# Dense attention: the value product in three float32r products with 512 moving columns

## The chip, the cores and the metric

The kernel runs on one core of a Trainium2 chip. A core has engines that run side by side, each with its own queue of instructions: TensorE (PE: matrix products and transposes; its weight loads are shown apart as PEld), VectorE (DVE), ScalarE (ACT), GpSimd (POOL), and SyncE (SP), which starts most transfers. They share the on-chip memory SBUF; PE writes into PSUM, eight banks of 512 fp32 columns by 128 partitions. The metric is the device time of one execution in microseconds (us), as the median of several runs.

## The reference

One encoder layer on 1,024 tokens with 1,024 features, all in float32: a normalisation, one projection, two attention mixers, an output projection, and a gated MLP with a convolution. The change lies in mixer A, dense attention with 8 query heads over 2 key/value heads of 64 features:

```
sc = jnp.einsum('bqkgd,bskd->bkgqs', qb, k, preferred_element_type=jnp.float32) * scale
p = jax.nn.softmax(sc, axis=-1)
return jnp.einsum('bkgqs,bskd->bqkgd', p.astype(v.dtype), v)
```

## The kernel before

All of SBUF is held in two arenas, `bigf` (float32) and `bigr` (float32r, a float32 that PE multiplies in a faster way with fewer bits), PSUM in one tile `ps`. A product that must keep float32's precision is made of float32r products: each operand is split into a high part (a copy that rounds to float32r) and a low part (the operand minus its high part), and high x high, high x low and low x high are added in PSUM.

The body is emitted twice, by `emit(True)` and, behind a condition, by `emit(False)`. The first is the bounded case: a bound on the scores, from the gains, lets the exponentials be taken without subtracting a row's maximum. With the given inputs the first alone runs to the end; the second is skipped.

Mixer A (`a_main`, from 210 to 391 us) is a loop over 16 groups `g`. A group is one block of 128 tokens by one key/value head with its 4 query heads, so 512 query columns. For each of 8 blocks `kt` of 128 keys, a step,

- two float32r products make the scores of 128 keys by 512 queries in a PSUM bank (L701, L702), four banks in turn;
- ACT takes their exponential into one of three slots of `bigf` (L704);
- two steps later, the value product (`pv`, L696): four float32 products, in each of which 128 query columns of the exponentials are the weights and 65 columns move, the 64 features of the value and a column of ones that yields the softmax's denominator. A float32 product is two instructions. The result lies with queries on partitions.

The last two value products of a group and its normalisation (`o_norm`, L721 and L722: DVE's reciprocal of the denominators and the product with them) are handed as `tail` to the next group and done in its first steps. `prep` brings the next group's queries: a split (L650 on ACT, L651 on DVE), then four transposes on PE (L182) and a copy out of PSUM on ACT (L667). `late` and `spread` put other work into the loop: in groups 0 and 1 what is left of the projection's rotary sums (DVE L433, L524, L527; POOL L294 and L517), in groups 5 to 9 mean squares for mixer B's queries (ACT L547, DVE L499, a root on ACT at L505 with a change of its function table), the preparation of output weights (ACT L955, DVE L960), fills (L1069); in groups 10 to 13 four normalisations (DVE L563, L564, then POOL's gain L530). Groups 14 and 15 also prepare mixer B (from L762 on).

Each instruction stands in the program in the order in which the functions are called; a scheduler then sets the order on every engine's queue, taking an instruction earlier or later by its own estimates of when the operands are ready. An engine works its queue in order. So the order around the change is found in the built program, not in the text of the kernel alone.

Of the kernel before, what the change touches and what calls it, by code (L numbers as in the profile page):

```python
# [14 lines left out]
AF = mybir.ActivationFunctionType  # L15
# [17 lines left out]
O_IDF = 0  # L33
# [93 lines left out]
def tile_encoder_layer(ctx, tc, x, w_in, gains, outg, norm1_g, norm2_g, w_out, w_up, conv_w, conv_b,  # L127
# [14 lines left out]
    def emit(bounded):  # L142
# [7 lines left out]
        def f(off, n):  # L150
            return bigf[:, off:off + n]
# [11 lines left out]
        def fp(off, *dims):  # L163
            return raw_ap(bigf[:, off:off + 1], dims)
# [49 lines left out]
        def qab(tt):  # L214
            return O_QAB + 1024 * tt
# [130 lines left out]
            act(rp(R_KHA + 256 * u, [128, 2], [1024, 2], [1, 128])[0:64], pb[0:64], AF.Copy)  # L346

        def v_fetch():
            gp.memset(fp(F_VA + 64, [66, 16]), 1.0)
            for kv in range(2):  # L350
                dma(fp(F_VA + 66 * kv, [132, 8], [1, 64]),
                    kvscr[:, :, 128 + 64 * kv:192 + 64 * kv].rearrange("t p c -> p t c"))

        def v_scale():

            vec.tensor_copy(f(SM_SS1, 1), f(SM_MC, 1))
            vec.tensor_copy(f(SM_SS1, 8), f(SM_R1, 8))
            for t in range(8):
                v = fp(F_VA + 132 * t, [66, 2], [1, 64])
                act(v, v, AF.Copy, scale=f(SM_SS1 + t, 1))  # L360

        def fill_k():
            for i in range(4):
# [320 lines left out]
            return [nat, first] + [lambda i=i: mx(i) for i in range(4)] + [last]  # L684

        def a_main(g, prep, tail, late, plan, late_plan):

            b, kv = divmod(g, 2)
            q2 = R_Q2A + 512 * (g % 2)
            ql = R_QLA + 512 * (g % 2)  # L690
            ob = 6 + g % 2
            slots = {}

            def pv(kt):
                for i in range(4):
                    mm(bank(ob, 65, 66 * i), f(slots[kt] + 128 * i, 128), f(F_VA + 132 * kt + 66 * kv, 65),  # L696
                       start=(kt == 0 and i == 0), stop=(kt == 7), skip_group_check=True)

            for kt in range(8):
                st = (2, 3, 0, 1)[kt % 4] if bounded else 2 + kt % 2  # L700
                mm(bank(st), r(R_K2A + 1024 * kv + 128 * kt, 128), r(q2, 512), start=True, stop=False)  # L701
                mm(bank(st), r(R_KHA + 1024 * kv + 128 * kt, 128), r(q2 if bounded else ql, 512), start=False, stop=True)  # L702
                slots[kt] = p_slots()[0]
                act(f(slots[kt], 512), bank(st), AF.Exp)  # L704
# [12 lines left out]
            return [lambda: pv(6), lambda: pv(7), lambda: o_norm(ob, 66, qab(b) + 256 * kv, ([64, 4], [1, 64]))]  # L717

        def o_norm(t, step, dst, dims):
# [507 lines left out]
            if g > 3 and fills:  # L1227
                fills.pop(0)(qab((g - 1) // 2) + 256 * ((g - 1) % 2))
        for t in tail:
            t()  # L1230
        take(prep, 99)

        first, steps_of = b_prep(1)
# [442 lines left out]
```

## Time and profile before

| | us |
|---|---|
| median of three runs | 1301.46 (1300.12 to 1302.01) |
| the profiled execution | 1300.51 |
| its span | 1298.7 |
| dense attention within it | 210 to 391 |

| engine | busy in the whole span | busy from 210 to 391 us |
|---|---|---|
| PE | 1236.4 | 181.00 |
| DVE | 908.5 | 41.16 |
| ACT | 637.4 | 101.81 |
| POOL | 391.8 | 23.22 |

The span is that of the engines' work; the execution's time has 1.8 us more around it. A row of a timeline gives start, duration, engine, line, what is written and read, and in brackets how long the engine had been idle and what ended that. Rows of one engine overlap: a matrix product is shown with its latency, so the distance from start to start is what one costs, and ACT and DVE begin an instruction before the last has ended where the two don't depend on each other. A row of groups gives count, busy time, mean ns of one and the idle time before it. A row of stretches gives the length, busy time and number of instructions of PE, PEld, DVE, ACT and POOL in that order, then the granted TensorE clock, the share of the DMA engines and GB/s.

### The profile page before, as it was taken

What the parts mean: (1) busy time and instruction counts of PE and PEld (TensorE: products, weight loads), DVE (VectorE), ACT (ScalarE), POOL (GpSimd) and SP (SyncE); (2) the same over time, 40 slices, a digit from 0 to 9 for tenths busy, and PEclk for the clock granted to TensorE, in tenths of its full rate; (3) what the DMA queues carried; (4) which work ended last, traced back from release to release, by engine and by line L of the source; (5) the groups of instructions that cost most, each with busy time, mean ns of one, the idle gap of its engine ahead of it and who ended that gap; (6) DMA issues with size and microseconds to landing.
All of it is one profiled execution on the core that took longest, in us unless ns stands there. A gap on an engine that the chain in (4) does not pass through costs nothing.

```text
span 1298.7 us, 18774 instructions
## 1 busy us (share of the span) xinstructions
PE 1236.4 (95%) x7063; PEld 1061.5 (82%) x7063; DVE 908.5 (70%) x1270; ACT 637.4 (49%) x1001; POOL 391.8 (30%) x300
## 2 busy tenths in 40 slices
PE   7999999999998889999999999999999998889996
PEld 7999998999997777888788888888888886657885
DVE  5988685124107779656999999999999964657672
ACT  7856554566556566535544453444443442234430
POOL 1610143000212230011465675665675530000000
PEclk9999999999999899999999999999999998999998
DMA  7126303000014444413222223232223357448970
GB/s 264 54 84 156 88 5 75 24 17 17 9 25 100 106 107 115 156 65 106 74 105 91 92 93 122 94 117 90 91 96 122 122 183 282 166 148 277 315 242 36
DMA packets 120935, 147.12 MB, mean 113 GB/s; under 512 B 51009, under 2 KB 79489, under 8 KB 120321
## 3 DMA queue, kind: packets, MB, share of 16 engines
q1 hardware_dynamic: 119617, 141.10, 33.6%
q0 software_dynamic: 1216, 4.72, 1.7%
q8 instruction: 57, 0.93, 0.3%
q14 instruction: 45, 0.37, 0.1%
HBM read 107.25 MB, written 33.82 MB: 109 GB/s over the span
## 4 chain that ended last, share of the span: by engine, by line
PE 55%; DVE 18%; issue 4%; DMA 4%; ACT 3%; POOL 1%; SPq 0%; ACTq 0%; DVEq 0%; POOLq 0%
PE ps L696 8%; PE ps L1349 6%; PE ps L1351 6%; PE ps L1350 6%; DVE bigf L1382 6%; PE ps L1481 4%; PE ps L1482 4%; PE ps L1480 4%; PE ps L701 3%; PE ps L702 2%; DVE bigf L1353 2%; PE ps L1004 2%; PE ps L1006 2%; PE ps L1005 2%; DVE bigr L1333 2%
## 5 line engine op out<-in xcount | busy, mean ns | idle before, releaser
L1349 PE MATMUL ps<-bigr 128*128 128x512 f32 x616 | 241.0, 391 | 6.5 <-DVE bigf L1353 5.9
L1350 PE MATMUL ps<-bigr 128*128 128x512 f32 x616 | 239.7, 389 | 0.0
L1351 PE MATMUL ps<-bigr 128*128 128x512 f32 x616 | 239.7, 389 | 0.0
L1382 DVE SCALAR_TENSOR_TENSOR bigf<-bigf 128x768 f32<-128x768 f32 (+1 forms) x176 | 178.8, 1074 | 26.5 <-ACT bigf L1380 26.4
L1332 ACT ACTIVATE bigr<-bigf 128x512 fp32r<-128x512 f32 x154 | 93.2, 625 | 139.3 <-POOL bigf L1324 70.4
L1460 ACT ACTIVATE bigr<-bigf 128x1024 fp32r<-128x1024 f32 x77 | 80.5, 1058 | 148.9 <-DMA bigf<-gscr 57.1
L1349 PEld LDWEIGHTS ps<-bigr 128*128 128x128 f32 x616 | 115.6, 188 | 35.1 <-DVE bigf L1353 9.3
L696 PEld LDWEIGHTS ps<-bigf 128*128 128x128 f32 x1024 | 131.9, 191 | 9.3 <-issue 0.3
L1351 PEld LDWEIGHTS ps<-bigr 128*128 128x128 f32 x616 | 115.6, 188 | 24.2
L1350 PEld LDWEIGHTS ps<-bigr 128*128 128x128 f32 x616 | 115.7, 188 | 23.5
L1461 DVE TENSOR_TENSOR bigr<-bigf,bigr 128x1024 fp32r<-128x1024 f32 x77 | 93.2, 1222 | 57.0 <-ACT bigr L1460 46.8
L1480 PE MATMUL ps<-bigr 128*128 128x512 f32 x308 | 114.1, 401 | 16.6 <-ACT bigr L1460 16.4
L696 PE MATMUL ps<-bigf 128*128 128x65 f32 x1024 | 129.1, 269 | 0.0
L421 PE MATMUL ps<-bigr 128*128 128x256 f32 x448 | 127.3, 284 | 1.2 <-ACT bigf L300 1.2
L1333 DVE TENSOR_TENSOR bigr<-bigf,bigr 128x512 fp32r<-128x512 f32 x112 | 125.3, 1136 | 3.2 <-ACT bigr L1332 2.5
L422 PE MATMUL ps<-bigr 128*128 128x256 f32 x448 | 126.9, 283 | 0.1
L423 PE MATMUL ps<-bigr 128*128 128x256 f32 x448 | 126.7, 283 | 0.0
L1481 PE MATMUL ps<-bigr 128*128 128x512 f32 x308 | 122.6, 400 | 1.4 <-DVE bigr L1461 0.9
L1482 PE MATMUL ps<-bigr 128*128 128x512 f32 x308 | 121.3, 395 | 0.0
L704 ACT ACTIVATE bigf<-ps 128x512 f32<-128x512 f32 x128 | 76.1, 597 | 78.9 <-PE ps L702 77.9
L421 PEld LDWEIGHTS ps<-bigr 128*128 128x128 f32 x448 | 85.8, 192 | 1.8 <-ACT bigf L300 1.6
L422 PEld LDWEIGHTS ps<-bigr 128*128 128x128 f32 x448 | 85.9, 192 | 0.3 <-DVE bigr L405 0.3
(215 smaller groups left out, 2441.8 us busy)
## 6 DMA issues: line engine op xcount, KB each, us to landing
bigf<-w_down SPq DMA_DIRECT2D x99, 256.0 KB, 3.7
bigf<-w_up SPq DMA_DIRECT2D x44, 512.0 KB, 3.6
bigf<-gscr SPq DMA_DIRECT2D x77, 256.0 KB, 3.7
gscr<-bigf SPq DMA_DIRECT2D x33, 512.0 KB, 2.6
bigf<-w_in SPq DMA_DIRECT2D x8, 1024.0 KB, 5.5
bigf<-x SPq DMA_DIRECT2D x15, 512.0 KB, 7.1
bigf<-w_out SPq DMA_DIRECT2D x8, 512.0 KB, 3.6
bigr<-bigr POOLq DMA_DIRECT2D x8, 512.0 KB, 4.7
```

Of the source, the lines that this page charges most:

```text
L421: mm(o, ah, wh, start=(k == 0 and t % 2 == 0 and n != 2), stop=False, skip_group_check=True)
L422: mm(o, ah, wl, start=False, stop=False, skip_group_check=True)
L423: mm(o, al, wh, start=False, stop=(k == 3), skip_group_check=True)
L696: mm(bank(ob, 65, 66 * i), f(slots[kt] + 128 * i, 128), f(F_VA + 132 * kt + 66 * kv, 65), start=(kt == 0 and i == 0), stop=(kt == 7), skip ...
L1333: (gp if n in (2, 4) and m > 3 else vec).tensor_tensor(rp(o + 512, [128, 4], [1, 128]), src, rfp(o, [128, 4], [1, 128]), op=OP.subtract)
L1349: mm(bank(b), wh, th, start=(k == 0 and n in (1, 5, 6, 7)), stop=False, skip_group_check=True)
L1350: mm(bank(b), wh, tl, start=False, stop=False, skip_group_check=True)
L1351: mm(bank(b), wl, th, start=False, stop=(k == 3), skip_group_check=True)
L1382: vec.scalar_tensor_tensor(f(a + o, n), f(i + d, n), w_, f(a + o, n), op0=OP.mult, op1=OP.add)
L1480: mm(o, ah, r(d, 512), start=(q == 0 and n in (1, 5, 2)), stop=False, skip_group_check=True)
L1481: mm(o, ah, r(d + 1024, 512), start=False, stop=False, skip_group_check=True)
L1482: mm(o, al, r(d, 512), start=False, stop=(q == NQ - 1), skip_group_check=True)
```

## The change

In the bounded case mixer A gets a function of its own. The exponentials become the moving operand, 512 columns at a time, and the values the weights (66 columns: 64 features, and two columns of ones). For that both are split: the values once ahead of the loop (`R_VA`, L364 and L365), the exponentials in every step, the high part by a copy, on DVE in steps 1, 4 and 7 and on ACT in the others, the low part by a subtraction on DVE (L763). The value product is now three float32r products (L738) and comes three steps behind. Its result lies with features on partitions, so at a group's end DVE copies it out of PSUM (`o_copy`, L741), PE turns it back with four float32 transposes (`o_turn`, L746), and the normalisation reads the turned result. These parts of the tail are done in steps 0 to 4 of the next group.

```diff
+R_VA = R_XT + 9248
+F_OT = O_F + 3616
...
         def v_fetch():
-            gp.memset(fp(F_VA + 64, [66, 16]), 1.0)
+            gp.memset(fp(F_VA + 64, [66, 16], [1, 2]), 1.0)
...
+            if bounded:
+                act(r(R_VA, 1056), f(F_VA, 1056), AF.Copy)
+                vec.tensor_tensor(r(R_VA + 1056, 1056), f(F_VA, 1056), rf(R_VA, 1056), op=OP.subtract)
...
         def a_main(g, prep, tail, late, plan, late_plan):
+            if bounded:
+                return a_main_bounded(g, prep, tail, late, plan, late_plan)
...
+        def a_main_bounded(g, prep, tail, late, plan, late_plan):
+
+            b, kv = divmod(g, 2)
+            q2 = R_Q2A + 512 * (g % 2)
+            ob = 6 + g % 2
+            ot = F_OT + 512 * (g % 2)
+            slots = {}
+
+            def pv(kt):
+                _, ph, pl = slots[kt]
+                v = R_VA + 132 * kt + 66 * kv
+                for i, (w, p) in enumerate(((v, ph), (v + 1056, ph), (v, pl))):
+                    mm(bank(ob)[0:66], r(w, 66), r(p, 512), start=(kt == 0 and i == 0), stop=(kt == 7 and i == 2))
+
+            def o_copy():
+                vec.tensor_copy(f(ot, 512)[0:66], bank(ob)[0:66])
+
+            def o_turn():
+                t = next_tr()
+                for i in range(4):
+                    nc.tensor.transpose(bank(t, 66, 128 * i), f(ot + 128 * i, 128)[0:66], f(O_IDF, 66)[0:66])
+                o_norm(t, 128, qab(b) + 256 * kv, ([64, 4], [1, 64]))
+
+            def last():
+                pv(7)
+                o_copy()
+
+            for kt in range(8):
+                st = (2, 3, 0, 1)[kt % 4]
+                mm(bank(st), r(R_K2A + 1024 * kv + 128 * kt, 128), r(q2, 512), start=True, stop=False)
+                mm(bank(st), r(R_KHA + 1024 * kv + 128 * kt, 128), r(q2, 512), start=False, stop=True)
+                p, ph, pl = slots[kt] = p_slots()
+                act(f(p, 512), bank(st), AF.Exp)
+                if kt in (1, 4, 7):
+                    vec.tensor_copy(r(ph, 512), f(p, 512))
+                else:
+                    act(r(ph, 512), f(p, 512), AF.Copy)
+                vec.tensor_tensor(r(pl, 512), f(p, 512), rf(ph, 512), op=OP.subtract)
+                take(prep, plan[kt])
+                take(late, late_plan[kt])
+                if tail:
+                    step = tail.pop(0)
+                    if step:
+                        step()
...
+                if kt >= 3:
+                    pv(kt - 3)
+
+            return [lambda: pv(5), lambda: pv(6), last, None, o_turn]
```

The function that is left for the other case keeps its lines; below it every line of the kernel after stands 61 or 62 lines lower, and between the values' split and it 5 lower (L524 is L529, L563 is L568).

Where the instructions stand now is shown at three places. First PE's queue in a group with no other work, around the transposes of the next group's queries: L701 and L702 are the scores, L696 the value product, L182 the transposes. Before:

```order
L182 MATMUL ps<-bigr 128x128 x4
L696 MATMUL ps<-bigf 128x65 x4
L701 MATMUL ps<-bigr 128x512
L702 MATMUL ps<-bigr 128x512
L696 MATMUL ps<-bigf 128x65 x4
```

And now, with L755 and L756 for the scores, L738 for the value product, L184 for the queries' transposes and L746 for the turn of the last group's result:

```order
L755 MATMUL ps<-bigr 128x512
L756 MATMUL ps<-bigr 128x512
L184 MATMUL ps<-bigr 128x128 x4
L746 MATMUL ps<-bigf 128x66 x4
L738 MATMUL ps<-bigr 66x512 x3
```

Each step has three products of 512 columns where four (eight instructions) of 65 stood, and the turn stands right behind the queries' transposes.

Second, DVE's queue from the end of the projection into group 1: L433 are sums of the projection, L524 and L527 the rotary sums, which wait for POOL's L294, L651 the split of queries, L721 and L722 the normalisation of a result. Before:

```order
L433 TENSOR_TENSOR bigf<-ps,bigf 128x4x256
L433 TENSOR_TENSOR bigf<-bigf 128x4x256
L524 TENSOR_TENSOR bigf<-bigf 128x4x256
L651 TENSOR_TENSOR bigr<-bigf,bigr 128x4x64
L527 TENSOR_TENSOR bigf<-bigf 128x4x256
L721 RECIPROCAL bigf<-ps 128x4
L722 TENSOR_TENSOR bigf<-ps,bigf 128x256
```

And now, where these are L438, L529 and L532, with the copies L760 (high parts) and subtractions L763 (low parts):

```order
L438 TENSOR_TENSOR bigf<-bigf 128x4x256
L763 TENSOR_TENSOR bigr<-bigf,bigr 128x512
L760 COPY bigr<-bigf 128x512
L763 TENSOR_TENSOR bigr<-bigf,bigr 128x512 x2
L529 TENSOR_TENSOR bigf<-bigf 128x4x256
L763 TENSOR_TENSOR bigr<-bigf,bigr 128x512
L760 COPY bigr<-bigf 128x512
L763 TENSOR_TENSOR bigr<-bigf,bigr 128x512 x3
L532 TENSOR_TENSOR bigf<-bigf 128x4x256
```

The rotary sum L529 stands behind the splits of three steps and ahead of all later ones, so these wait with it for POOL.

Third, DVE's queue at two of the four normalisations of groups 10 to 13. L543 is a copy of one column that only sets the order, L563 copies the factors, L564 multiplies, and POOL's L530 follows it. Before:

```order
L199 TENSOR_SCALAR bigf<-bigf 128x64
L563 COPY bigf<-bigf 128x16
L564 TENSOR_TENSOR bigf<-bigf 128x4x256
L543 COPY bigf<-bigr 128x1
L563 COPY bigf<-bigf 128x16
```

And now (L548, L568 and L569 are the same three):

```order
L763 TENSOR_TENSOR bigr<-bigf,bigr 128x512
L548 COPY bigf<-bigr 128x1
L568 COPY bigf<-bigf 128x16
L569 TENSOR_TENSOR bigf<-bigf 128x4x256
L763 TENSOR_TENSOR bigr<-bigf,bigr 128x512
L760 COPY bigr<-bigf 128x512
```

Each normalisation now stands between the splits of two steps.

More of the change, by code (lines that the diff above doesn't have):

```diff
@@ L717, in a_main @@
             return [lambda: pv(6), lambda: pv(7), lambda: o_norm(ob, 66, qab(b) + 256 * kv, ([64, 4], [1, 64]))]
+        def a_main_bounded(g, prep, tail, late, plan, late_plan):
[36 more added lines that the diff above has]
+                        step()
+                now = f(qab((g - 1) // 2) + 256 * ((g - 1) % 2), 1) if 0 < kt < 7 else \
+                    rf(R_Q2A + 512 * ((g + (kt == 7)) % 2), 1)
+                for step in spread.pop((g, kt), []):
+                    step(now)
+                if kt >= 3:
+                    pv(kt - 3)
+            return [lambda: pv(5), lambda: pv(6), last, None, o_turn]
         def o_norm(t, step, dst, dims):
@@ L1229, in emit @@
         for t in tail:
-            t()
+            if t:
+                t()
         take(prep, 99)
```

## The prediction

> **What bounds the kernel now.** I read four views in this order: the page's busy shares, the busy times of the stretch in which dense attention runs, the waits in that stretch, and its instructions in order of time.
>
> ```profile
> PE 1236.4 (95%) x7063; PEld 1061.5 (82%) x7063; DVE 908.5 (70%) x1270; ACT 637.4 (49%) x1001; POOL 391.8 (30%) x300
> 210.00:391.00 181.00, 181.00 (x1362) 168.81 (x1360) 41.16 (x96) 101.81 (x179) 23.22 (x27) 1.00 0.07 18
> ACT bigf L704 <- PE ps L702: 77.9, 110, 3.3
> ...
> 243.60 0.47 PE L701 MATMUL ps<-bigr 128*128 128x512 f32 x1
> 243.92 0.39 PE L702 MATMUL ps<-bigr 128*128 128x512 f32 x1
> 244.15 1.00 PE L696 MATMUL ps<-bigf 128*128 128x65 f32 x8
> 244.96 0.47 PE L701 MATMUL ps<-bigr 128*128 128x512 f32 x1
> 245.27 0.39 PE L702 MATMUL ps<-bigr 128*128 128x512 f32 x1
> ...
> 245.76 0.60 ACT L704 ACTIVATE bigf<-ps 128x512 f32<-128x512 f32 x1 [0.46 <-PE ps L702]
> ```
>
> The second row is the stretch from 210 to 391 us, all sixteen groups: TensorE (PE) is busy for all 181.00 us at clock 1.00, VectorE (DVE) for 41.2, ScalarE (ACT) for 101.8, GpSimd (POOL) for 23.2. ACT's idle time is ended by PE (third row). So PE alone sets this stage, and the stage is 14% of the span. The timeline gives its pitch: one step of 128 keys takes 244.96 - 243.60 = 1.36 us, two score products and eight fp32 instructions of the value product. 128 steps make 174.1 us; the other 6.9 are transposes.
>
> **PE's work after the change.** A step becomes five products of 512 columns. Their pitch, and that of a product with 66 weight columns, stand elsewhere in the trace, and so does the price of four transposes:
>
> ```profile
> 569.67 0.39 PE L1004 MATMUL ps<-bigr 128*128 128x512 f32 x1
> ...
> 572.64 0.39 PE L1005 MATMUL ps<-bigr 128*128 128x512 f32 x1
> ...
> 411.64 0.40 PE L919 MATMUL ps<-bigr 128*66 128x256 f32 x2
> ...
> 377.55 0.49 PE L701 MATMUL ps<-bigr 128*128 128x512 f32 x1
> ...
> 378.11 0.46 PE L182 MATMUL ps<-bigr 128*128 128x128 f32 x4
> ...
> 379.29 0.48 PE L701 MATMUL ps<-bigr 128*128 128x512 f32 x1
> ...
> 409.48 0.46 PE L936 MATMUL ps<-bigf 65*128 65x65 f32 x4
> 409.75 0.36 PE L892 MATMUL ps<-bigr 128*128 128x256 f32 x1
> ```
>
> Fourteen products start between 569.67 and 572.64: 2.97/13 = 0.229 us each. Two 66-column products of 256 take 0.40 us where one takes 0.28, a pitch of 0.12: the narrow weights run at the rate of the columns that move. I take 0.23: 128 x 5 x 0.23 = 147.2 us. Four transposes lengthen a step by 1.74 - 1.36 = 0.38 (377.55 to 379.29); the four fp32 ones of L936 take 0.27. The sixteen turns of the result (after.py L746) cost 0.27 to 0.38 each; I take 0.35, since the turn also splits a run of products as the first row does: 5.6. With the 6.9 carried over, PE needs 159.7 us: **21.3 us less**, if it never waits.
>
> **What ACT and DVE take on.** ACT gets five copies a group, DVE three copies, eight subtractions and one copy out of PSUM.
>
> ```profile
> 378.37 0.60 ACT L704 ACTIVATE bigf<-ps 128x512 f32<-128x512 f32 x1 [0.16 <-PE ps L702]
> 378.87 0.59 ACT L784 ACTIVATE bigr<-ps 128x512 fp32r<-128x512 f32 x1
> ...
> L650 ACT ACTIVATE bigr<-bigf 128x512 fp32r<-128x512 f32 x2 | 1.3, 628 | 0.0
> ...
> 395.37 0.43 DVE L906 CAST bigr<-bigf 128x512 fp32r<-128x512 f32 x1
> 395.71 0.68 DVE L900 TENSOR_TENSOR bigf<-ps,bigf 128x512 f32<-128x512 f32 x1
> 396.31 0.68 DVE L907 TENSOR_TENSOR bigr<-bigf,bigr 128x512 fp32r<-128x512 f32 x1
> 396.91 0.42 DVE L906 CAST bigr<-bigf 128x512 fp32r<-128x512 f32 x1
> ```
>
> On ACT an independent successor starts 0.50 us after an exponential; a copy of the same tile must wait out its 0.60. Per group: 5 x (0.63 + 0.52) + 3 x 0.50 + 0.8 for the query work = 8.1 us. On DVE the pitches are 0.34 for a copy and 0.60 for a subtraction: 8 x 0.60 + 3 x 0.36 + 0.6 + 0.9 for normalising and the query split = 7.4. PE needs 159.7/16 = 9.98. So in a group with nothing else PE still sets the pace and all of the ACT and DVE work is hidden.
>
> How long can a part be late before PE stands? From the start of L702's product to that of its exponential are 0.49 us (245.27, 245.76); then 0.60 + 0.63 + 0.68 for exponential, high part, low part, and three hand-overs of about 0.05: 2.55 us. PE comes to the product that needs the low part after its own eighteen products, 18 x 0.23 = 4.14 us. The cover is **1.6 us**. What keeps DVE or ACT from the splits for longer stalls PE, and PE gives nothing back.
>
> **Where it is longer.** DVE and POOL hinder each other:
>
> ```profile
> 397.63 1.26 POOL L766 TENSOR_TENSOR bigr<-bigf,bigr 128x512 fp32r<-128x512 f32 x1 [2.72 <-ACT bigr L765]
> ...
> 397.85 1.60 DVE L907 TENSOR_TENSOR bigr<-bigf,bigr 128x512 fp32r<-128x512 f32 x1
> ...
> 319.10 0.17 DVE L563 COPY bigf<-bigf 128x16 f32<-128x16 f32 x1
> ...
> 321.88 1.19 DVE L563 COPY bigf<-bigf 128x16 f32<-128x16 f32 x1
> ...
> 320.67 2.37 POOL L530 TENSOR_TENSOR bigf<-bigf 128x1024 f32<-128x1024 f32 x1 [86.13 <-DVE bigf L564]
> ...
> 213.23 3.37 POOL L294 TENSOR_TENSOR bigf<-bigf 128x128 f32<-128x128 f32 x8 [11.66 <-DVE bigf L433]
> ...
> 216.63 1.23 DVE L524 TENSOR_TENSOR bigf<-bigf 128x1024 f32<-128x1024 f32 x1 [3.55 <-POOL bigf L294]
> ```
>
> The subtraction of 0.68 takes 1.60 beside POOL's, and a copy of 0.17 takes 1.19: it ends at 323.07 where POOL ends at 323.04. I read this as one of the two standing until the other is through. Today DVE is 77% idle here and it costs nothing.
>
> *Groups 0 and 1.* DVE's rotary sums (after.py L529) wait for POOL's eight pieces and now stand in the queue ahead of splits. DVE is free at 213.1; three subtractions and a copy (2.46) and the eight pieces (3.37), one after the other, end at 218.9, not 216.6. The sum then takes 1.2, and the last split of the group comes six subtractions, two copies and another sum (5.4) later: 225.5. PE would be there after 12 pairs of scores, 25 products and a set of transposes, 11.7 us: at 222.1. That is 3.4 late. Group 1 has the same with one more POOL piece (1.28) and is late by about as much again: 7 us in both. Lower bound, if POOL's pieces don't hinder: 2.8; upper: 8.
>
> *Groups 10 to 13.* One normalisation each (L568, L569), and then POOL's L530.
>
> ```profile
> L564 DVE TENSOR_TENSOR bigf<-bigf 128x1024 f32<-128x1024 f32 x4 | 4.9, 1226 | 0.1
> L499 DVE TENSOR_REDUCE bigf<-bigf 128x16 f32<-128x1024 f32 x4 | 4.9, 1220 | 0.1
> ...
> L960 DVE SCALAR_TENSOR_TENSOR bigr<-bigf,bigr 128x1024 fp32r<-128x1024 f32 x2 | 2.6, 1276 | 0.0
> ...
> L505 ACT ACT_TABLE_LOAD x1 | 1.3, 1283 | 0.0
> ```
>
> The copy (0.17) and normalisation (1.15 by its pitch), one subtraction (0.68), POOL's 2.37 and the next subtraction (0.68) are 5.1 us for two parts; PE asks for two in 2 x 1.24 and has 1.6 in hand, 4.1. Late by 1.0 to 1.3. The second of the four comes five steps after the first, before DVE has caught up: 2.5. With 1.3 and 1.8 for the others: 7 us, between 0 (no hindrance: 1.3 is under the cover) and 15.6 (no cover: 4 x 3.9).
>
> *Groups 5 to 9.* L499 and L960 fall together twice with small copies (3.4 us around one subtraction), 0.5 late each; the two table loads around group 9's root (2 x 1.28 + 0.26, less 1.6) 1.2; small ones 0.8: 3 us, between 1 and 5. Groups 14 and 15: POOL pieces of 1.3 are under the cover, 0.5 for the turn that DVE holds at the end.
>
> *At no cost.* The split of the values (ACT and DVE, under 1.3 us each like the 1,024-wide rows above) falls into idle time before the stage:
>
> ```profile
> 207.35 0.42 ACT L650 ACTIVATE bigr<-bigf 128x256 fp32r<-128x256 f32 x1 [5.66 <-DVE bigf L433]
> ...
> 204.84 1.22 DVE L433 TENSOR_TENSOR bigf<-ps,bigf 128x1024 f32<-128x1024 f32 x1 [2.19 <-PE ps L423]
> ```
>
> Without that cover it would be 2.3 us. SP's queue moves one load of a table by a place; nothing waits for it.
>
> **Sum.** 21.3 saved less 7 + 3 + 7 + 0.5 = 17.5 leaves 3.8 us. The profiled execution took 1300.51 (span 1298.7), so 1296.7; the median of the runs, 1301.46, lies 0.95 higher: **1297.5**. A measurement of this kernel can tell about 0.2%, 2.6 us, from no change.
>
> **Rivals.** *No cover* (ends slower). If the hand-overs between ACT and DVE cost some tenths more than 0.05, or if ACT's exponential stands behind a copy, the 1.6 us are gone and every blockade counts in full: 15.6 instead of 7 in groups 10 to 13, 5 instead of 3, 8 to 10 instead of 7, 29 in all: 1309. It decides once the cover is below about 1 us. For it: eight of the sixteen groups hold a blockade. Against: the hand-over measured at 216.60 to 216.63 is 0.03.
>
> *PE stays the bound.* If POOL and DVE hinder each other only in part, the stalls shrink to 2.8 + 1 + 3 + 0.5, and the time is 1287. For it: POOL's eight pieces are short and leave gaps. Against: the two rows above.
>
> *The clock falls.*
>
> ```profile
> 395.00:400.00 5.00, 3.38 (x23) 2.77 (x23) 4.97 (x9) 3.74 (x9) 2.37 (x2) 1.00 0.54 109
> 400.00:405.00 5.00, 4.03 (x24) 3.31 (x25) 4.90 (x9) 1.58 (x3) 0.57 (x1) 0.66 0.36 90
> ```
>
> After five us with PE busy 3.38, the granted clock is 0.66 for the next five, 1.7 us of work at full clock. Groups 0 and 1 would hold such a stretch, groups 10 to 13 perhaps: two spells, 3.4 us, 1301: no change. The Trainium skill (TensorE: Matmul & The Clock Gate, Part 1: The HAM clock gate) says that the clock halves after at least one idle window of about 3.4 us; none of my stalls is that long, so by that rule this rival falls away and the sum stays. The trace doesn't agree: PE was never idle for 3.4 us between 395 and 405.
>
> The Trainium skill (SBUF — State Buffer, Who interferes with whom) says that a VectorE instruction with two SBUF inputs and a GpSimd one that reads SBUF exclude each other for the whole instruction. By that rule "PE stays the bound" falls away; the 1.60 us row agrees.
>
> **Chances.** Forecast 0.36, PE stays the bound 0.14 (both faster: 0.50), clock 0.18 (same), no cover 0.32 (slower). The forecast's own range is 1292 to 1299; over the cases 8 in 10 lie from 1287 (all hindrance gone) to 1309 (no cover).
>
> **What would show it.** In the profile after: the stage from the first L755 to the last L738 lasts some 177 us with PE busy about 160; quiet groups (2, 3, 4) take 10 us; PE's third product waits for DVE L763 in groups 0, 1 and 10 to 13; single L763 rows of 2 us and more beside L530. Quiet groups above 10.5 us, or waits in every group, would make the forecast wrong.

## The result, and the profile after

The changed kernel takes 1288.28 us (median of four, 1285.26 to 1291.21) where the kernel before, on the same chip, took 1300.79 (1299.90 to 1302.01): a ratio of 0.9899, 95% interval 0.9875 to 0.9923. A second comparison, with five more executions, gave 0.9897 (0.9879 to 0.9914). It is faster, by 12.5 us or 1.0%. The forecast, 1297.5, was 4.0 below the median shown before (its last step is off by 0.2: 1296.7 and 0.95 are 1297.7). The direction held and the time lies in the wide range, but the forecast's own range (1292 to 1299) missed it by 4 us, and the gain is three times the one forecast.

The profiled execution of the changed kernel took 1285.26 us (span 1283.5), 15.2 less than the profiled one of before. By stages, from the first product of each: 8.1 us of that are dense attention (181.24 to 173.17), 4.9 are mixer B (from 121.4 to 116.5), and 2.3 the down projection, from its first product to the end (251.0 to 248.6). The stages in between, the output projection (103.0) and the up projection (431.8), have not moved. The down projection takes 248.3 to 253.6 us in the profiles of this study, with either kernel's order, so its part isn't put down to the change.

Dense attention and mixer B before, as rows of stretches:

```profile
210.40:391.64 181.24, 181.24 (x1367) 169.05 (x1365) 41.60 (x98) 101.96 (x180) 23.22 (x27) 1.00 0.07 18
391.64:513.01 121.37, 107.73 (x787) 89.48 (x786) 98.32 (x190) 81.07 (x149) 31.66 (x26) 0.96 0.45 108
```

And after: first the page's busy shares, then the busy times of stretches cut at the first score product of groups 4, 5, 10 and 14, at the first product of mixer B and at the first of the output projection. The columns are those of the stretches shown before.

```profile
PE 1216.2 (95%) x6487; PEld 1000.8 (78%) x6487; DVE 1021.1 (80%) x1463; ACT 677.7 (53%) x1082; POOL 397.2 (31%) x300
```

```profile
210.33:253.64 43.31, 39.95 (x182) 26.13 (x181) 37.18 (x64) 33.03 (x63) 13.71 (x19) 0.96 0.10 23
253.64:263.46 9.82, 9.82 (x50) 6.86 (x48) 7.40 (x16) 8.29 (x16) 0.00 (x0) 1.00 0.00 0
263.46:313.48 50.02, 49.80 (x241) 33.86 (x239) 46.84 (x103) 46.32 (x83) 0.00 (x0) 1.00 0.07 22
313.48:360.22 46.74, 42.59 (x195) 28.04 (x194) 44.95 (x78) 34.36 (x64) 10.87 (x4) 0.96 0.03 7
360.22:383.49 23.27, 23.16 (x122) 15.94 (x121) 18.00 (x32) 19.22 (x37) 4.61 (x4) 1.00 0.17 35
383.49:500.00 116.51, 103.22 (x794) 86.55 (x794) 97.97 (x192) 81.04 (x149) 30.74 (x26) 1.00 0.46 113
```

Group 4, the second row, is a quiet one: PE never stands, 9.82 us, with DVE busy 7.40 and ACT 8.29. Four such groups would be 39.3. Groups 10 to 13 (fourth row) take 46.74, and DVE is busy for 44.95 of it. Groups 0 to 3 (first row) take 43.31; there 36.9 would be the time without stalls, by an estimate from group 4: group 0 has three value products and one turn less (2.4 us). Groups 2 and 3, which the prediction had also named as quiet, took 10.9 and 10.6 us.

What waits, over the whole stage, and the length of the two instructions that the prediction set against each other:

```profile
PEld ps L738 <- DVE bigr L763: 12.7, 19, 2.2
...
ACT bigf L758 <- DVE bigr L763: 11.1, 13, 2.2
DVE bigr L763 <- ACT bigr L762: 9.5, 19, 1.3
...
PE ps L738 <- DVE bigr L763: 4.5, 7, 1.8
```

```profile
L763 DVE TENSOR_TENSOR bigr<-bigf,bigr x128: 631/685/2886, 212.9 to 382.1; 128x512 fp32r<-128x512 f32 x128
...
L535 POOL TENSOR_TENSOR bigf<-bigf x4: 2687/2722/2743, 318.5 to 348.5; 128x1024 f32<-128x1024 f32 x4
```

The weight loads (PEld) of the value product wait for subtractions in 19 places, and in 7 of them PE itself stands, for 4.5 us in all. ACT waits for subtractions in 13 places: an exponential needs the slot that a subtraction three steps back still reads, so late subtractions hold the scores up as well. A subtraction takes 0.685 us as a rule and up to 2.886 beside POOL's gain (in group 13); the gain itself went from 2.37 to 2.72. The timeline around two of the four gains (DVE and POOL of group 10, then PE, then ACT of group 13) shows what stands:

```profile
317.19 1.22 DVE L569 TENSOR_TENSOR bigf<-bigf 128x1024 f32<-128x1024 f32 x1
318.33 3.47 DVE L763 TENSOR_TENSOR bigr<-bigf,bigr 128x512 fp32r<-128x512 f32 x2
321.72 0.68 DVE L741 COPY bigf<-ps 66x512 f32<-66x512 f32 x1
...
318.54 2.71 POOL L535 TENSOR_TENSOR bigf<-bigf 128x1024 f32<-128x1024 f32 x1 [78.06 <-ACT bigf L758]
...
322.45 0.46 PE L746 MATMUL ps<-bigf 66*128 66x66 f32 x4 [2.00 <-DVE bigf L741]
...
351.25 0.72 ACT L655 ACTIVATE bigr<-bigf 128x256 fp32r<-128x256 f32 x2 [2.39 <-POOL bigf L535]
```

Two subtractions take 3.47 instead of 1.29 us. The copy of the result (L741) stands behind them, and PE waits 2.00 us for it in front of the turn (L746), not in front of a third product. In group 13 ACT stands 2.39 us in front of the next query's split (L655) until POOL's gain is done: a wait that the prediction didn't have.

### The profile page after: what moved, and what is told of

Same layout as the page of the kernel before. It is cut to its first block, busy times and chain, and to the rows that moved or that the text cites. A ratio compares the mean times of both kernels' runs of the same rounds, so it can differ in the third digit from the quotient of the medians.

```text
span 1283.5 us, 17926 instructions
## 1 busy us (share of the span) xinstructions
PE 1216.2 (95%) x6487; PEld 1000.8 (78%) x6487; DVE 1021.1 (80%) x1463; ACT 677.7 (53%) x1082; POOL 397.2 (31%) x300
## 5 line engine op out<-in xcount | busy, mean ns | idle before, releaser
L1395 DVE TENSOR_TENSOR bigr<-bigf,bigr 128x512 fp32r<-128x512 f32 x112 | 125.2, 1135 | 3.2 <-ACT bigr L1394 2.6
L1544 PE MATMUL ps<-bigr 128*128 128x512 f32 x308 | 121.6, 396 | 0.0
L738 PE MATMUL ps<-bigr 128*66 128x512 f32 x384 | 114.8, 403 | 5.5 <-DVE bigr L763 4.5
L763 DVE TENSOR_TENSOR bigr<-bigf,bigr 128x512 fp32r<-128x512 f32 x128 | 92.5, 742 | 11.4 <-ACT bigr L762 9.5
```

The costliest lines, as they stand in the source:

```text
L1395: (gp if n in (2, 4) and m > 3 else vec).tensor_tensor(rp(o + 512, [128, 4], [1, 128]), src, rfp(o, [128, 4], [1, 128]), op=OP.subtract)
L1544: mm(o, al, r(d, 512), start=False, stop=(q == NQ - 1), skip_group_check=True)
```

## Experiments

All comparisons below are of dense attention by groups of the profiled executions, from first score product to first score product, and of mixer B from its first product to the first of the output projection. The theory is the prediction's: POOL's and DVE's instructions exclude each other, and what that makes late beyond a cover is paid by PE.

**Without the gain.**

```diff
-            spread[10 + i, 0] = [norm_at, lambda now, gain=gain: gain()]
+            spread[10 + i, 0] = [norm_at]
```

> The changed kernel without POOL's multiplication by the gain (L535) in groups 10 to 13: mixer B's queries lack that factor. DVE's normalisations (L568, L569) stay. In the changed kernel groups 10 to 13 took 46.7 us where a quiet group takes 9.82, so 7.4 us over, one half-clock stretch of up to 1.7 among it. My theory, that POOL's instruction keeps DVE's subtractions from running: groups 10 to 13 fall to 40 to 41.5 us, no single subtraction (L763) there takes over 1.5 us, and since PE no longer stands there before a stretch at half clock, that one goes too. Rival: DVE's own normalisations (1.2 + 0.2 us in one piece) fill the cover of 1.6 us, or groups 10 to 13 have too much DVE work anyhow: they stay above 44 us.

The stretch of groups 10 to 13, and the subtractions in it:

```profile
314.50:354.00 39.50, 39.50 (x194) 27.28 (x193) 36.68 (x78) 34.26 (x65) 0.00 (x0) 1.00 0.03 8
```

```profile
L763 DVE TENSOR_TENSOR bigr<-bigf,bigr x36: 661/686/694, 310.9 to 350.8; 128x512 fp32r<-128x512 f32 x36
```

39.5 us, PE busy throughout, no subtraction above 0.694 us, DVE busy 8.3 us less than with the gain (44.95). All 7.2 us go with POOL's four instructions, a little more than expected, though DVE's normalisations of 1.2 us are still there. PE's queue has the same order as with the gain. On DVE and ACT a few instructions that no longer wait for it (splits of the next queries, one copy of a result, one normalisation) stand some places earlier. The whole is 0.9838 of before (0.9816 to 0.9861).

**Without the rotary pieces.**

```diff
             def turn(i):
-                rot(so + ss * i, o + 1024 * i, 4, tab + ts * i)
+                None if kind == "qa" and late is not None else rot(so + ss * i, o + 1024 * i, 4, tab + ts * i)
```

> The changed kernel without POOL's rotary pieces (L296, eight in group 0 and eight in group 1): the rotation of the last eight query tiles is left out, DVE's sums (L529, L532) stay where they are in the queue and read what lies there. Every other engine keeps its order of instructions. In the changed kernel groups 0 to 3 took 43.3 us, of which a half-clock stretch accounts for up to 1.7; without any stall they would take 4 x 9.82 less three value products and one turn that group 0 does not do (2.4): 36.9. My theory, that DVE waits for POOL's pieces with the splits queued behind the sum, and the two hinder each other: 37 to 39 us, and the stretch at half clock, which follows PE's longest wait, goes. Rival: DVE's own sums, 2.4 us from the projection and 2.4 us of rotary sums in each of the two groups, are what PE waits for: 41 us or more.

Groups 0 to 3, and the first fifteen subtractions:

```profile
211.80:249.90 38.10, 37.57 (x182) 25.57 (x181) 35.93 (x64) 32.70 (x63) 3.52 (x3) 1.00 0.11 27
```

```profile
L763 DVE TENSOR_TENSOR bigr<-bigf,bigr x15: 679/685/1183, 214.4 to 230.1; 128x512 fp32r<-128x512 f32 x15
```

38.1 instead of 43.3 us, with DVE's sums in place and every other queue in the same order: 5.2 of the 6.4 us of stalls there are POOL's pieces. The rest isn't: group 3 still takes 10.5 us, with a third product that waits 0.46 us for its subtraction. No half-clock stretch is left in these groups. The ratio is 0.9861 (0.9836 to 0.9886).

**Both moved, nothing left out.** The rotary pieces run on DVE, the second eight in group 3; the gain becomes four POOL instructions.

```diff
-                rot(so + ss * i, o + 1024 * i, 4, tab + ts * i)
+                rot(so + ss * i, o + 1024 * i, 4, tab + ts * i, vec if kind == "qa" and late is not None else gp)
...
-            spread[10 + i, 0] = [norm_at, lambda now, gain=gain: gain()]
+            spread.update({(10 + i, 0): [norm_at]}) or spread.update({(10 + i, 1 + 2 * k): [lambda now, k=k, gain=gain: gain(k, 1)] for k in range(4)})
...
-        spread = {(1, 2): [lambda now: vec.tensor_copy(f(F_KN[0], 1), now)] + [lambda now, t=t: t() for t in turns[:3]],
+        spread = {(3, 1): [lambda now: vec.tensor_copy(f(F_KN[0], 1), now)] + [lambda now, t=t: t() for t in turns[:2]], (3, 2): [lambda now, t=t: t() for t in turns[2:3]],
```

> The changed kernel with both of POOL's disturbers moved: the sixteen rotary pieces run on DVE (the second eight, with their sums, in group 3 instead of 1), and the gain in groups 10 to 13 is four instructions of 256 columns on POOL instead of one of 1,024. Nothing is left out. My theory, cover and exclusion: a POOL piece of some 0.6 us keeps DVE waiting for less than the cover of 1.6 us, so groups 10 to 13 take 40 us as without the gain (they took 46.7), and DVE has room for eight pieces of about 0.2 us: groups 0 to 3 take 38 to 40 us (43.2 in the changed kernel). Dense attention from its first score product to mixer B: 162 to 165 instead of 173 us, the whole 8 to 11 us faster than the changed kernel: ratio to before 0.981 to 0.985. Rival: four short POOL instructions in a row hinder DVE as much as one long, and the pieces on DVE delay the splits as POOL did: groups 10 to 13 over 44 us, groups 0 to 3 over 42, ratio 0.988 to 0.992.

Groups 0 to 3 took 37.3 us: the first half is right. Groups 10 to 13 took 45.3, not 40: the second half fell, and the rival's "as much as one long" is right there, within 1.4 us of the changed kernel's 46.7. The timeline of groups 10 and 11, DVE's rows and then POOL's:

```profile
317.54 1.11 DVE L763 TENSOR_TENSOR bigr<-bigf,bigr 128x512 fp32r<-128x512 f32 x1
...
321.85 0.96 DVE L760 CAST bigr<-bigf 128x512 fp32r<-128x512 f32 x1
322.73 0.95 DVE L656 TENSOR_TENSOR bigr<-bigf,bigr 128x256 fp32r<-128x256 f32 x1
...
314.30 4.95 POOL L535 TENSOR_TENSOR bigf<-bigf 128x256 f32<-128x256 f32 x4 [63.46 <-DVE bigf L569]
321.48 1.05 POOL L535 TENSOR_TENSOR bigf<-bigf 128x256 f32<-128x256 f32 x1 [2.22 <-DVE bigf L569]
```

The two engines take turns: each POOL piece makes one DVE instruction longer by some 0.5 us (0.42 to 0.96 for a copy, 0.42 to 0.95 for a small subtraction), and four pieces in a row spread the same delay over several instructions. The busy times of groups 10 to 13:

```profile
309.29:354.60 45.31, 41.54 (x195) 26.66 (x194) 43.81 (x78) 34.49 (x64) 17.18 (x16) 1.00 0.03 7
```

DVE's busy time is 43.81 us; one long instruction a group made it 44.95, none 36.68. Dense attention up to mixer B took 166.7 us, more than the 162 to 165 expected. The ratio, 0.9845 (0.9823 to 0.9868), lies where it was expected, but it comes mostly from groups 0 to 3: 6.0 us there, 1.4 in groups 10 to 13.

**Two steps behind instead of three.** The value product of a step comes one step earlier (`pv(kt - 2)`, with the tail shorter by a part).

> The changed kernel with the value product two steps behind its scores instead of three: PE has five products (1.15 us) less to do before it needs a step's low part, so the cover falls from the 1.6 us of my estimate to about 0.45. DVE's, ACT's and POOL's work is the same. My theory: quiet groups keep 9.8 to 10.1 us, since the chain of 2.55 us still ends before PE asks (3.0 us), and each stretch with a blockade costs 1.15 us more, some six to nine of them: dense attention up to mixer B 180 to 183 us instead of 173. Rival 1, that the hand-overs are dearer and the cover is already near nothing: quiet groups rise above 10.5 us. Rival 2, that DVE's sum of work in these groups and not its lateness sets the time: dense attention stays within 2 us of 173.

Dense attention up to mixer B took 174.9 us, 1.7 more than 173.2: groups 0 to 3 44.4 (43.3), groups 10 to 13 48.1 (46.7), quiet groups 9.2 to 9.9. The two runs of late groups:

```profile
211.19:255.58 44.39, 40.64 (x185) 26.42 (x184) 36.64 (x63) 33.75 (x63) 14.76 (x19) 0.96 0.09 23
315.57:363.70 48.13, 40.77 (x194) 26.61 (x193) 45.59 (x76) 36.53 (x67) 10.48 (x4) 1.00 0.03 6
```

The expected 180 to 183 fell. The growth of 1.1 and 1.4 us is about what the five products (1.15 us) cost once in each run of late groups, and not once for each block. The time, within 2 us of 173, is also the one that the second rival gave, DVE's sum of work; the run with all high copies on ACT, below, tests that rival by itself. PE's queue has another order throughout in this run, so it doesn't measure the cover alone.

**Idle sums on DVE.**

```diff
+        [spread.setdefault((g, 4), []).append(lambda now, n=n: (vec.tensor_copy(f(F_VA, 1), now), vec.tensor_reduce(f(F_VA + 1024, n), fp(F_VA, [0, n], [1, 512]), axis=AX.X, op=OP.add))) for g, n in ((4, 3), (11, 2), (12, 4), (13, 6))]; load_v(0)
```

> The changed kernel without POOL's gain, as before, and with four idle sums on DVE that nobody reads (each preceded by a copy of one column that ties it to its group): 1,536 columns (1.8 us) in group 4, 1,024 (1.2 us) in group 11, 2,048 (2.4 us) in group 12 and 3,072 (3.6 us) in group 13; the last three groups also hold a normalisation of 1.2 us. Without them these groups took 9.83, 9.78, 9.83 and 9.78 us. My theory, a cover of 1.6 us: the lengthening is the excess over it, 0 to 0.3 in group 4, 0 to 0.3 in group 11, 0.8 to 1.3 in group 12 (with what spills into the next), 2.0 to 2.4 in group 13 (with group 14). Rival, a cover near nothing: 1.8, 1.2, 2.4 and 3.6. Rival, that any lateness is made up because PE has work to do out of order: below 0.3 each.

```profile
341.20 2.29 DVE L1255 TENSOR_REDUCE bigf<-bigf 128x4 f32<-128x2048 f32 x1
...
353.32 3.34 DVE L1255 TENSOR_REDUCE bigf<-bigf 128x6 f32<-128x3072 f32 x1
```

Groups 4, 11, 12 and 13 took 9.82, 9.78, 9.81 and 9.83 us: not one was longer. Only group 14, behind the block of 3.34, was, by 1.2. That is near the figure of the third theory (below 0.3 each), but it doesn't measure the cover of the kernel as it was: PE's queue has another order here, with products of scores and values changed about around the sums. What it shows is that late work on DVE around which the order is written cost little; POOL's hold on DVE, in the order written for the changed kernel, is paid.

**Idle products on POOL.** Here PE, DVE and ACT keep the order that they have without the gain.

```diff
+        [spread.setdefault((g, k), []).append(lambda now, n=n: (gp.tensor_copy(f(F_VA, 1), now), gp.tensor_tensor(fp(F_VA, [64, n], [1, 64]), fp(F_VA, [64, n], [1, 64]), fp(O_GB, [0, n], [1, 64]), op=OP.mult))) for g, k, n in ((4, 4, 16), (6, 4, 8), (11, 0, 8), (12, 0, 16), (13, 4, 16))]; load_v(0)
```

> The changed kernel without POOL's gain in groups 10 to 13, and with five idle products of the same kind on POOL that nobody reads: 1,024 columns in group 4, 512 in group 6, 512 in group 11, 1,024 in group 12 and 1,024 in group 13, that of group 12 beside the normalisation as the gain was, the others tied to the middle of a group. PE, DVE and ACT keep their order of instructions. Without them these groups took 9.83, 9.82, 9.78, 9.83 and 9.78 us. A product of 1,024 columns on POOL took 2.7 us, one of 512 some 1.3. Theory of the prediction, a block is paid for beyond a cover of 1.6 us: +1.0 to 1.2 in groups 4 and 13, nothing in group 6, +0.5 to 1 in group 11, +2 in group 12. Rival, the sum: a group lasts as long as DVE's work and POOL's together, where that is over 9.8 us (7.4 for the splits and the result, 1.4 for the normalisation in groups 11 to 13): +0.3 in group 4, 0 in group 6, +0.3 in group 11, +1.7 in groups 12 and 13. Where a group is lengthened, what spills into the next counts with it.

```profile
263.46 2.41 POOL L1255 TENSOR_TENSOR bigf<-bigf 128x1024 f32<-128x1024 f32 x1
...
333.73 2.79 POOL L1255 TENSOR_TENSOR bigf<-bigf 128x1024 f32<-128x1024 f32 x1
...
355.70 2.41 POOL L1255 TENSOR_TENSOR bigf<-bigf 128x1024 f32<-128x1024 f32 x1
```

The rows of groups 5 and 12, which took 10.0 and 9.8 us without the products:

```profile
265.31:275.95 10.64, 10.20 (x49) 6.68 (x48) 10.00 (x19) 9.05 (x17) 0.56 (x1) 1.00 0.01 2
336.55:347.76 11.21, 10.04 (x49) 6.77 (x48) 10.90 (x22) 7.91 (x16) 0.00 (x0) 1.00 0.00 1
```

Measured over what the groups took without them, the spill into the next group with it: the first +0.6 (group 5), the 512 columns of group 6 +0.4 (in group 7), of group 11 +0.3, the one beside the normalisation in group 12 +1.4, the last +0.2 to 0.3. Neither list fits. Two lone blocks of 2.41 us cost 0.2 to 0.6, as if the cover were 1.8 to 2.2 us; yet blocks of 1.30 and 1.76 us cost 0.4 and 0.3, which a cover of that size would hide. So no single cover fits: what a block costs hangs on where it falls, and the one with the normalisation in front (1.2 us) cost most, 1.4.

**All high copies on ACT in groups 10 to 13.** The gain stays whole on POOL.

```diff
-                if kt in (1, 4, 7):
+                if kt in (() if 10 <= g < 14 else (1, 4, 7)):
```

> The changed kernel, with POOL's gain, but in groups 10 to 13 all high copies are made by ACT, none by DVE: three copies of 0.36 us a group leave DVE and three of 0.52 us come to ACT (8.1 to 9.7 us a group, still under PE's 9.82). POOL's block of 2.7 us is as it was. Theory, the sum: DVE has 7.4 + 1.4 and POOL 2.7 to do one after the other, 11.5 us a group, as the three last of these groups took on average (11.5); without the copies 10.4: groups 10 to 13 take 42 to 43.5 us instead of 46.7. Rival, the block alone: each block is paid for beyond the cover, whatever DVE does in the rest of the group: 45.5 to 47.

```profile
314.63:360.23 45.60, 42.10 (x195) 28.06 (x194) 40.12 (x66) 38.42 (x74) 10.80 (x4) 0.96 0.03 7
```

Groups 10 to 13 take 45.6 us with DVE busy for 40.12 of it; the ratio is 0.9895 (0.9875 to 0.9916), as for the changed kernel. DVE had 4.8 us less to do, and the groups were 1.1 us shorter. So my second theory, that DVE is simply full there, fell as well. (ACT's 4.1 us more are not what held them up: in the last of these runs, below, ACT is nearly as busy and the groups take 39.8 us.) What PE and ACT waited for in them:

```profile
PEld ps L746 <- DVE bigf L741: 3.2, 2, 2.5
PEld ps L738 <- DVE bigr L763: 3.0, 6, 1.0
PE ps L746 <- DVE bigf L741: 2.6, 2, 2.0
ACT bigr L655 <- POOL bigf L535: 1.9, 1, 1.9
```

Most of the time goes to the block itself, and through three places: a third product that waits for its subtraction, the turn that waits for the copy behind it, and ACT's query split that waits for POOL. The four blocks don't cost alike: the groups took 13.9, 9.8, 10.6 and 11.3 us.

**No POOL beside DVE at all.** As the kernel with both moved, but the gain is one DVE product about a group after its normalisation, and in groups 10 to 13 ACT makes seven of eight high copies.

```diff
-                if kt in (1, 4, 7):
+                if kt in ((4,) if 10 <= g < 14 else (1, 4, 7)):
...
-            def gain():
-                gp.tensor_tensor(q3, q3, fp(O_GB, [0, 4], [0, 4], [1, 64]), op=OP.mult)
+            def gain(now):
+                [tick(F_KN[1] + 256, now), vec.tensor_copy(f(F_KN[1] + 256, 64), f(O_GB, 64)), vec.tensor_tensor(q3, q3, fp(F_KN[1] + 256, [0, 4], [0, 4], [1, 64]), op=OP.mult)]
...
-            spread[10 + i, 0] = [norm_at, lambda now, gain=gain: gain()]
+            spread.update({(10 + i, 0): [norm_at], (10 + i, 4): [gain]})
```

> The changed kernel with nothing left out, in which POOL no longer works beside DVE: the rotary pieces run on DVE in groups 0 and 3 (there, groups 0 to 3 took 37.3 us with them), the gain of groups 10 to 13 runs on DVE as one product of 1,024 columns (1.2 us and small copies of 0.5) about a group after its normalisation, and in groups 10 to 13 DVE makes one high copy of eight, ACT the others. Theory, the sum: DVE has some 7.4 + 1.4 + 1.7 - 0.7 = 9.8 us a group there, no more than PE: groups 10 to 13 take 39.5 to 41 us (46.7 in the changed kernel, 45.3 with the gain in four pieces on POOL), dense attention up to mixer B 160 to 162.5 us instead of 173, and the whole, with mixer B between 116.5 and 120, 1274 to 1279: ratio to before 0.978 to 0.983. Rival, ACT with seven copies and DVE's products of 1.2 us in a row keep PE waiting: over 43 us in groups 10 to 13, ratio 0.984 or more.

```profile
310.74:350.51 39.77, 39.74 (x194) 27.25 (x193) 38.38 (x81) 37.43 (x70) 0.00 (x0) 1.00 0.00 1
```

As expected: 39.8 us for these groups, PE busy throughout with DVE at 38.4 and ACT at 37.4; dense attention up to mixer B 161.2; a ratio to before of 0.9816 (0.9798 to 0.9834). The median, 1279.23 us, is 0.2 over the upper end. This beats both kernels: its interval lies below that of the changed kernel.

**Mixer B: the same kernels again.**

> The kernel before, unchanged, to see whether its mixer B is always as long as in the profile of before. There mixer B, from its first product (L892) to the first of the output projection (L1004), took 121.4 us and held three stretches of 3.41 us at a granted clock of 0.50 (from 401.3, 432.0 and 449.1); in the changed kernel it took 116.5 us and held none. Theory A, the clock: the stretches come by the phase of a grid of 3.41 us that is not tied to the program, so another execution has another number of them, and mixer B takes 116.5 us plus 1.3 to 1.7 for each: any value from 116.5 to 122. Rival B, the order of the work: the change has moved some instructions of mixer B, and the kernel before always takes 121.4, plus or minus 0.5, with three such stretches in the same places.

> The changed kernel, unchanged. Theory A, the clock: another execution has its half-clock stretches elsewhere; dense attention takes 172.7 us less or more a stretch of 1.7 us (it held two), mixer B 116.5 plus 1.3 to 1.7 for each that falls there; the single times spread over 1285 to 1291 as the first four did, and the ratio over five rounds is 0.990, plus or minus 0.002. Rival B, the order: dense attention 172.7, mixer B 116.5, each within 0.5, with the stretches at the same places in the program, at 221 and 323.5 us.

> The kernel before, with the value product left out in nine of the 128 steps (groups 2, 3 and 4, key blocks 2, 4 and 6): dense attention is about 8 us shorter, as in the changed kernel, and mixer B keeps the order of instructions of before. So far mixer B took 121.4 and 121.6 us in the kernel before, each time with three stretches of 3.41 us at half clock, and 116.5, 117.9, 117.5 and 119.3 in four executions with the changed order, with 0, 1, 1 and 2 of them. Theory A, alignment: the number of stretches hangs on how mixer B lies to the grid of 3.41 us, and with another start it changes: mixer B below 120 us. Theory B, order of the work: mixer B stays at 121 to 122 us with three stretches. Either way its length is 116.5 plus 1.5 to 1.7 for each stretch.

(The last leaves out the value products by one line, `range(0 if g in (2, 3, 4) and kt in (2, 4, 6) else 4)`.) The second execution of the kernel before took 121.6 us in mixer B, with three stretches; that of the changed kernel 117.9, with one. Its dense attention, with no stretch at half clock, took 173.0 us, against 173.2 with two. The shortened kernel took 173.2 us in dense attention, 8.1 less, and 122.7 in mixer B, again with three stretches. First two pairs of neighbouring stretches of 3.41 us of the kernel before, then a pair at the same place of the changed kernel:

```profile
397.89:401.30 3.41, 1.67 (x16) 1.35 (x14) 3.41 (x5) 1.24 (x3) 2.68 (x2) 1.00 0.36 82
401.30:404.71 3.41, 3.06 (x18) 2.47 (x16) 3.31 (x7) 1.13 (x2) 0.00 (x0) 0.50 0.20 58
428.61:432.02 3.41, 2.25 (x21) 1.67 (x20) 3.41 (x7) 0.58 (x1) 0.67 (x1) 1.00 0.82 170
432.02:435.43 3.41, 3.19 (x18) 2.71 (x17) 3.41 (x8) 1.14 (x3) 0.00 (x0) 0.50 0.18 58
```

```profile
391.52:394.93 3.41, 2.19 (x16) 1.62 (x15) 2.93 (x5) 1.26 (x4) 1.69 (x2) 1.00 0.52 135
394.93:398.34 3.41, 3.41 (x29) 2.97 (x28) 1.38 (x2) 3.41 (x8) 1.28 (x1) 1.00 0.02 4
```

A stretch in which PE is busy 1.67 or 2.25 of 3.41 us is followed by one at half clock; one with 2.19, in the changed kernel, is not. Mixer B and its half-clock stretches in all thirteen profiles:

| order of mixer B's instructions | profiles | half-clock stretches | mixer B, us |
|---|---|---|---|
| that of before | before, again, shortened | 3, 3, 3 | 121.4, 121.6, 122.7 |
| that of the changed kernel | eight | 0, 0 | 116.5, 116.5 |
| | | 1, 1, 1 | 117.5, 117.9, 117.9 |
| | | 2, 2, 2 | 119.0, 119.1, 119.3 |
| that of "two steps behind" and "idle sums on DVE" (a third order) | two | 3, 3 | 122.1, 122.7 |

So mixer B is 116.5 us and 1.0 to 2.1 for each stretch. Both theories hold a part. The shortened kernel before starts mixer B 7.8 us earlier and lies otherwise to the grid, yet has its three at the same places (9.7, 40.4 and 57.5 us after its start before, 11.2, 41.9 and 59.0 there): that is the order. It shows most plainly where executions lie alike to the grid. Mixer B began 0.57, 0.26 and 2.44 us after an edge of the grid in the three profiles with the order of before, with three stretches each time. The profiles of the changed order that come nearest, at 0.70, 0.29 and 2.55 us, held one, two and none. Within the changed order the number runs from 0 to 2 without any change to mixer B: that is the alignment. Which of the moved instructions makes the changed order less prone was not tested and stays open.

## Why the prediction was right, and where it was off

| term | predicted | measured in the profile after |
|---|---|---|
| PE's work in dense attention | -21.3 | -24.1: 16 x 9.82 = 157.1 from 181.2 |
| stalls from groups 0 and 1 | +7 | +6.4: 43.3 - 36.9, groups 0 to 3 |
| stalls in groups 5 to 9 | +3 | +0.9: 50.0 - 49.1 |
| stalls in groups 10 to 13 | +7 | +7.4: 46.7 - 39.3 |
| groups 14, 15 and the end | +0.5 | +1.2 |
| sum for dense attention | -3.8 | -8.2 by the terms; -8.1 by the stage |
| mixer B | 0 | -4.9 in this pair of profiles |

*PE's work.* The pitch of 0.23 us and the sum of five products were right; the carried transposes and the turn were sized at 0.78 us a group and cost 0.66 or less (9.82 - 40 x 0.229). The quiet group 4 took 9.82, 10.0 predicted, with ACT at 8.29 (8.1) and DVE at 7.40 (7.4). But of the three groups that the prediction named as quiet, groups 2 and 3 took 10.9 and 10.6 us, over the 10.5 that it gave as a sign against itself. Without the rotary pieces group 2 takes 9.8, so its part is lateness carried over from group 1; group 3 still takes 10.5, a wait for a subtraction that the sum didn't have.

*Groups 0 and 1.* Right in cause, shown by the run without the pieces, and within its bounds (2.8 to 8) in size: 5.2 us go with them, 7 predicted; the 6.4 in the table hold group 3's wait as well.

*Groups 10 to 13.* Right in cause (all of it goes without POOL's gain) and in size, but the size is in part luck. The prediction's terms for the four groups were 1.3, 2.5, 1.3 and 1.8 us; against the run without the gain, the profiled execution paid 3.7, 0.5, 1.3 and 1.7, the second one 2.2, 2.0, 1.3 and 1.7. The step "PE asks for two in 2 x 1.24 and has 1.6 in hand" knew one place of waiting; there are three, and the first of the four groups lost 2.0 us in front of the turn. Nor is there one cover of 1.6 us: idle blocks of 1.3 and 1.8 us cost 0.3 to 0.4, blocks of 2.4 us 0.2 to 0.6. That the two engines stand for each other was read rightly from 1.60 and 1.19 us; the Trainium skill (SBUF — State Buffer, Who interferes with whom) says so for a VectorE instruction with two SBUF inputs, and the subtraction at up to 2.886 us agrees.

*Groups 5 to 9.* Mis-sized: 3 predicted, 0.9 measured. An explanation that fits is that the order was written around these bursts, as in the run with idle sums on DVE; no run left the bursts out, so it isn't shown.

*"No cover".* Fell: in the quiet group 4 PE never waits, although its DVE and ACT work is all there, and with the value product one step earlier, 1.15 us of PE's work, dense attention grew by only 1.7 us.

*"PE stays the bound".* Its time, 1287, was nearly met, but by luck: POOL's hindrance is whole (6.4 and 7.4 us). What came out smaller were PE's own work and the stalls of groups 5 to 9, and mixer B's 4.9 us were in neither its account nor the forecast's.

*"The clock falls".* Two half-clock stretches came, one in group 1 and one in group 10, where the rival put them, and cost nothing. The dip before the first and the stretch itself:

```profile
217.44:220.85 3.41, 1.61 (x7) 0.83 (x6) 2.87 (x5) 1.21 (x3) 0.51 (x2) 1.00 0.00 0
220.85:224.27 3.42, 3.42 (x10) 2.01 (x9) 3.42 (x6) 2.41 (x5) 0.00 (x0) 0.50 0.00 0
```

The second execution of the changed kernel cut the same dip in two, with 2.35 and 2.30 us of PE, and had no stretch there; groups 0 to 3 took 43.2 us against 43.3, groups 10 to 13 46.7 in both, here at full clock throughout:

```profile
212.39:255.56 43.17, 38.58 (x181) 25.17 (x180) 37.39 (x64) 32.98 (x63) 13.57 (x19) 1.00 0.10 24
315.38:362.10 46.72, 41.35 (x195) 26.96 (x194) 45.26 (x78) 34.46 (x65) 10.81 (x4) 1.00 0.03 7
```

PE waits for DVE there anyway, so that its lost 1.7 us lie in the wait. The rule of the Trainium skill (TensorE: Matmul & The Clock Gate, Part 1: The HAM clock gate), an idle window of about 3.4 us, would have ruled both out; PE was never idle for more than 2.0 us at a time in dense attention, so its word "idle" doesn't agree. Its window of 3413 ns that runs freely does: the stretches of one execution lie whole multiples of 3.413 us apart (30 of them from 220.83 to 323.23 us here), and where they lie to the start of mixer B differs from execution to execution, as above.

*The step that failed for the rest* is one that is not there: the sum stopped at the end of dense attention. The fence on the clock quoted a half-clock stretch in mixer B of the kernel before, yet it was used only as a sign of what might come. Counted, mixer B held three of them, 3 x 1.7 = 5.1 us of PE's clock, and the change, which moved mixer B and its order, lost one to three of them: 4.9 us in the profiled pair, 3.7 in the second pair. The other part of the miss lies in dense attention, 4.3 us: chiefly PE's own work (2.8 more saved than forecast) and groups 5 to 9 (2.1).

## What to carry to other kernels

Before giving an engine new work, look at what runs beside it on an engine that excludes it, and count the block at every instruction that stands in the same queue behind the blocked one, copies for later stages and splits on a third engine too; cutting the block into four pieces won 1.4 of 7.2 us here; moving the work to DVE, with some of DVE's copies handed to ACT, won all but 0.2. List every half-clock stretch of the trace and the dip ahead of it, in all stages: in mixer B each was worth 1 to 2 us that a change elsewhere won, and where PE waited for DVE anyway they cost nothing. Ask too what the scheduler's order takes into account: idle sums on DVE changed PE's queue and cost little, idle products on POOL changed no other queue and were paid in part.

## What was not expected of the hardware

- Half clock needs no idle stretch: in mixer B of the kernel before, PE never stood for more than 0.89 us. In mixer B, grid stretches with PE busy from 0.83 to 2.43 of 3.41 us were followed by half clock, but those with 2.06 to 2.08 near its end, in eight profiles, were not. So PE's busy time alone doesn't tell which dip is followed.
- DVE and POOL pass the way to each other after every instruction: four POOL products of 256 columns took 4.95 us from first to last, one of 1,024 took 2.71, and DVE lost about as much to both (7.1 and 8.3 us in four groups).
- A copy with one input in SBUF (L760) is held beside POOL as well: 0.42 to 0.96 us for 512 columns.
